# A decoder layer whose planner is given other costs, and whose gated stages get more groups of seven products

## The chip, the cores and the metric

The kernel runs on one core of a Trainium2 chip. The metric is device time in microseconds. Before the change it is 1747.77 us, the median of three runs (1747.45 to 1747.9). TensorE (PE in the profile) multiplies, VectorE (DVE) and ScalarE (ACT) prepare operands and finish results, SyncE (SP) issues the weight loads, GpSimd (POOL) issues the accumulating stores of the residual.

## The reference, cut to what matters

One layer on 256 tokens of width 2048, in float32: a gated feed-forward stage, a mixer of two kinds of attention, and a second gated stage. D_FF is 5632.

```
h = x + 0.5 * swiglu(rms_norm(x, g1), w_gate1, w_up1, w_down1)
u = rms_norm(h, g_mix);  proj = u @ w_in          # split into heads of two kinds
o = concat(rms_norm(o_fox), rms_norm(o_swa)) @ w_out;  h = h + o
y = h + 0.5 * swiglu(rms_norm(h, g2), w_gate2, w_up2, w_down2)
swiglu(x, g, u, d) = (silu(x @ g) * (x @ u)) @ d
```

## The kernel before, in words

**Products.** Every factor of a matrix product is split into a high and a low part, and a product is three matmuls of 128x512: high by high, low by high, high by low (`mm3`, L326 to L328). ScalarE makes the high part of a weight tile by a cast, VectorE the low part by subtracting the high one (L389).

**Units and groups.** `ffn()` is called once per gated stage. The 5632 columns are cut into 11 units of 512. A unit multiplies the normed input by the unit's gate and up weights in eight groups; a group is one pair of blocks of the input (pair 0 to 7) and one weight tile of 128x2048, 1 MB. After each unit but the first comes the previous unit's "down" block, four groups with the third weight matrix; the last two down blocks come together.

**Two kinds of group.** A plain group, D, is eight products: ScalarE casts the tile (L407), VectorE makes 2048 columns of low part (L389). A group of seven, S, computes the same 2x2 block product with seven products, in the manner of Strassen and Winograd. For it VectorE forms sums of weight blocks: an outer addition of 1024 columns (L437), two inner ones of 512 (L444, L445). ScalarE casts 1536 columns of the plain tile (L421) and twice 1024 of the sums (L423, L425). VectorE makes a low part of 1536 columns and one of 2048 (both L389). The first three products use the plain blocks, the other four the sums. The left side needs sums too, which `form_of` makes once per pair and stage, in the first unit in which that pair is in an S group: five steps on VectorE into `sqh` (L564 to L569), casts on ScalarE (L573, L574), then two low parts, `fu` and `u`. A unit with S groups ends with eight combination steps on VectorE (L626), then the gate (L641, L649) and the transposes and split of the result `hT` (L507, L389).

**Which unit has which kinds.** `UNITS` says it, one letter a group, the same for both stages: unit 0 is eight D, unit 1 "DDSSDSDD", unit 2 "DSSSSSDD", the other eight "SDSSSSSD". The S groups of a unit take the lowest pairs.

**What sets the order.** The code of a stage makes tasks, and `arrange` puts them in order, before anything is issued, by simulating the five engines with a cost for each task. `cast(n)` and `sub(n)` are the costs of a cast and an addition or subtraction of n columns, `LAG` the time from a task's end to its users' start; other costs are numbers in the code. A task is taken when its inputs are there and its buffers free, the earliest `due` first. Each engine then runs its list in the order found. The buffers of a stage are 3 raw tiles, 2 of sums, 5 of high and 5 of low parts.

**Vectors.** A tile `vec` of 128x226 with gains, biases and rotary factors is loaded at the start by ScalarE's queue (L256). Its first 64 columns are what the gated stages use, and the mixer uses the rest: the rotary tables (L938), the negated sinks `nsink` (L950), the forget bias and the gains of the other heads. SP loads the mixer's other constants, `mst`, at L881.

Of the kernel before, what the change touches and what calls it, by code (L numbers as in the profile page):

```python
# [9 lines left out]
F32 = mybir.dt.float32  # L10
# [7 lines left out]
P = 128  # L18
# [6 lines left out]
HD = 64  # L25
# [12 lines left out]
UNITS = ["D" * 8, "DDSSDSDD", "DSSSSSDD"] + ["SDSSSSSD"] * (NB - 3)  # L38
# [5 lines left out]
F2_ORDER += [(2, "whiy", F32R)] * (NHI - 2 - FREE2) + [(3, "wloy", F32R)] * (NLO - 2 - FREE2) + [(0, "rawy", F32)] * (NRAW - 3)  # L44

# [32 lines left out]
LAG = 0.06  # L78
# [3 lines left out]
def cast(n):  # L82
    return 0.2 + 0.00084 * n


def sub(n):
    return 0.16 + 0.00104 * n
# [9 lines left out]
def arrange(tasks, pools):  # L97
# [102 lines left out]
def hybrid_layer(ctx: ExitStack, tc: tile.TileContext, a: dict, out: bass.AP):  # L200
# [55 lines left out]
    nc.scalar.dma_start(vec, a["vec"])  # L256
# [101 lines left out]
    def ffn(pool, u, wgu, wd, slots, banks, rstd, held=None, first=None, lead=None, done=None, out=None):  # L358
# [58 lines left out]

        def seven(src):
# [49 lines left out]
        def group(kind, src, held, stat, need, form=None, pieces=1, last=False):  # L468

            new, w, free = seven(src) if kind == "S" else whole(src, pieces)  # L470
# [62 lines left out]
        def squares_of(ssq, c, need, due):  # L533

            ends = []
            for t in range(NT):
                q = task("act", 0.84, None, need[t], due, take={"sq": 1})
# [11 lines left out]
        count = [k.count("S") for k in UNITS]  # L549

        def form_of(p, need, due):

            tile_, over = fu[p], u(2 * p)[:, :, P:SEQ]
# [35 lines left out]
        def unit(b):  # L589

            kinds, ns = UNITS[b], count[b]
            pair = {"S": iter(range(ns)), "D": iter(range(ns, 8))}
            held, hs, sq3 = {}, [], []
            for n, kind in enumerate(kinds):
                p = next(pair[kind])
                if b == 0 and first is not None:
                    first[0](p, task, ready)
                if kind == "S" and p not in forms:
                    fresh[p] = len(main)
                    form_of(p, used[p] + [x for k in (2 * p, 2 * p + 1) for x in ready.get(k, ())], len(main) - 4)  # L600
# [18 lines left out]
            if ns:  # L619
# [4 lines left out]
                def step(o_, key, in1, op, need, due, free=True):  # L624
                    return task(
                        "dve", 0.69, lambda: tt(out=o_(), in0=bank_of(held[key]), in1=in1(), op=op), need + [held[key]["last"]], due,  # L626
# [12 lines left out]
            for t in range(NT):  # L639
                src = (lambda t=t: s_tile()[:, t, :]) if ns else (lambda t=t: bank_of(R(t, 0)))  # L640
                a = task("act", 0.73, lambda t=t, src=src: nc.scalar.activation(  # L641
# [7 lines left out]
                f = task("dve", 0.7, lambda t=t, src=src: stt(  # L649
# [9 lines left out]
            def finish(k, v, x):  # L659
# [6 lines left out]
                l = task("dve", 0.69, lambda: low(rows_tile()[:, :, 1, :], v(), rows_tile()[:, :, 0, :]), [c], due + 4)  # L666
# [12 lines left out]
        def down(blocks, final):  # L679
# [5 lines left out]
            for i, (cp, b, c) in enumerate(todo):  # L685
                final_of_cp = cp not in [x[0] for x in todo[i + 1 :]]
                if left[b] == 4:
# [3 lines left out]
                    "D", wd[cp][2 * b + c], held[cp], lambda k, t, b=b, c=c: halves(rows[b][:, 2 * c + k], t),  # L691
# [9 lines left out]
        def settle(cp, held, final, later):  # L701

            due, c0, ends = len(main), 2 * cp * 512, []
            for t in range(NT):
                if not final:
                    pair = []
                    for j in range(2):
                        def run(t=t, j=j, pair=pair, held=held):
# [3 lines left out]
                            "act", 0.63, run, [held[t, j]["last"]] + pair, due + t + 4 * j, take={"st": 1} if j == 0 else (),  # L712
# [101 lines left out]
    with tc.tile_pool(name="f1", bufs=1) as fp:  # L814
# [10 lines left out]
        def before(p, task, ready):  # L825
# [12 lines left out]
            for j in range(2):  # L838
                k = 2 * p + j
                gain = vec[:, V_G1 + k : V_G1 + k + 1]  # L840
                c = task("act", 0.46, lambda j=j, k=k, gain=gain: nc.scalar.mul(
                    u1(k)[:, 0, :], xs[i][:, p % 4, j], gain
                ), [ld], 8 * p - 4)
                l = task("dve", 0.48, lambda j=j, k=k, gain=gain: nc.vector.scalar_tensor_tensor(
# [33 lines left out]
    with tc.tile_pool(name="mix", bufs=1) as mp:  # L878
        ap_ = mp
        mst = mp.tile([P, C_END - C_ONE], F32, name="mst")  # L880
        nc.sync.dma_start(mst, a["cst"][:, C_ONE:])  # L881
        ones, tri = mst[:, :P], mst[:, C_TRI - C_ONE : C_TRI - C_ONE + P]
# [55 lines left out]
        def rope_tables(name, gcol):  # L938
            g = vec[:, gcol : gcol + HD]
# [10 lines left out]
        nc.vector.tensor_scalar_mul(nsink, vec[:, V_SINK : V_SINK + NH], -1.0)  # L950
# [93 lines left out]
        def fox_mm(hf, i):  # L1044
# [11 lines left out]
            out=z, in0=prs[:, :, 0:NH], in1=vec[:, V_BF : V_BF + NH].unsqueeze(1).broadcast_to([P, NT, NH]), op=ALU.add  # L1056
# [117 lines left out]
        def fox_rows(hf, i, pr, rf):  # L1174
# [3 lines left out]
            for t in range(NT):  # L1178
# [11 lines left out]
                for jj in range(2):  # L1190
                    bt = small_ps()
                    for j in range(4):
# [8 lines left out]
                        vec[0 : HD + 2, gcol : gcol + 1],  # L1201
# [85 lines left out]
    with tc.tile_pool(name="f2", bufs=1, reuse_waits=REUSE) as fp:  # L1287
        slots, fu = [[], [], [], []], []
        for i, nm, dt in F2_ORDER:
            if i == 4:  # L1290
                fu += [fp.tile([P, 3, 2, P], F32R, name="fu%d" % p) for p in range(max(k.count("S") for k in UNITS))]
# [90 lines left out]
```

## Time and profile before

| | us |
|---|---|
| median of three runs | 1747.77 |
| the profiled execution | 1747.29 |
| its span, first to last instruction | 1745.0 |
| TensorE busy | 1734.7 |
| VectorE busy | 1510.2 |
| ScalarE busy | 1058.4 |
| GpSimd busy | 73.8 |

The span is 2.29 us shorter than the execution's own time. Stage 1 runs from the start to about 700 us, the mixer to about 1055 us, stage 2 to the end. The granted TensorE clock is 1.000. A busy time is a sum of instruction durations with overlaps counted once; TensorE's matmuls overlap, so the distance from one start to the next is shorter than a duration. A row of a timeline gives the start from the span's beginning, the duration, the engine and line, output and inputs, and in brackets how long the engine had been idle and what ended that.

### The profile page before, as it was taken

The page shows a single profiled execution, that of the slowest core. Times are in us where ns is not written, and L with a number is a line of the kernel's source. Part 1 is how long each engine was busy: PE and PEld are TensorE (multiplying, and loading weights), DVE is VectorE, ACT ScalarE, POOL GpSimd, SP SyncE. Part 2 cuts the span into 40 slices and gives each one's busy share as a digit, 9 for nine tenths or more (in the row PEclk, how much of TensorE's full clock was granted, in tenths as well). Part 3 has the DMA queues.
Part 4 walks back from the last instruction along what each step waited for, and adds up shares of the span by engine and source line. Part 5 has one row for each costly group of instructions (what it writes and reads, how often), then busy time and mean ns, then how long its engine had stood idle before and what let it go on. Part 6 is the DMA issues. An engine that isn't in the chain of part 4 may idle for free.

```text
span 1745.0 us, 21056 instructions
## 1 busy us (share of the span) xinstructions
PE 1734.7 (99%) x8052; PEld 1444.1 (83%) x8052; DVE 1510.2 (87%) x1640; ACT 1058.4 (61%) x1217; POOL 73.8 (4%) x94
## 2 busy tenths in 40 slices
PE   9999999999999999999999999999999999999999
PEld 6888888888888888998788888888888888888887
DVE  7899999998999996668777769799999999999994
ACT  7566566666666654655766656556666566656661
POOL 0000000000000000000000000000000000000000
PEclk9999999999999999999999999999999999999999
DMA  9676677678678664564444456577678578667763
GB/s 345 221 234 237 215 247 246 212 241 250 229 220 266 227 237 154 166 210 153 139 146 138 135 191 241 201 209 241 217 227 259 220 233 265 215 226 246 256 214 121
DMA packets 73141, 377.49 MB, mean 216 GB/s; under 512 B 7760, under 2 KB 16464, under 8 KB 39504
## 3 DMA queue, kind: packets, MB, share of 16 engines
q1 hardware_dynamic: 62064, 337.09, 53.8%
q0 software_dynamic: 10688, 38.80, 11.5%
q8 instruction: 63, 1.03, 0.2%
q14 instruction: 38, 0.31, 0.1%
q10 hardware_dynamic: 288, 0.25, 0.0%
HBM read 336.27 MB, written 2.10 MB: 194 GB/s over the span
## 4 chain that ended last, share of the span: by engine, by line
PE 98%; DMA 1%; DVE 0%; ACT 0%; issue 0%; SPq 0%; DVEq 0%
PE acc L327 25%; PE acc L326 25%; PE acc L328 25%; PE sm L328 6%; PE sm L326 6%; PE sm L327 6%; PE acc L507 1%; PE sm L1025 1%; PE sc L1214 1%; DMA rawx<-in_wgu 1%; PE sm L1031 1%; PE sm L1193 0%; PE sm L507 0%; DMA raw<-in_wgu 0%; PE sc L1139 0%; PE sm L1032 0%
## 5 line engine op out<-in xcount | busy, mean ns | idle before, releaser
L326 PE MATMUL acc<-whi,u 128*128 128x512 f32 (+1 forms) x690 | 263.4, 383 | 0.9 <-DVE s L989 0.9
L327 PE MATMUL acc<-wlo,u 128*128 128x512 f32 (+1 forms) x690 | 263.4, 382 | 0.6 <-DVE wlo L389 0.5
L328 PE MATMUL acc<-whi,u 128*128 128x512 f32 (+1 forms) x690 | 262.0, 381 | 0.0
L243 DVE TENSOR_TENSOR wlo<-raw,whi 128x1024 fp32r<-128x1024 f32 (+1 forms) x112 | 128.9, 1154 | 75.1 <-ACT whi L242 74.5
L242 ACT CAST whi<-raw 128x1024 fp32r<-128x1024 f32 (+1 forms) x112 | 111.0, 991 | 96.8 <-PE acc L328 88.1
L389 DVE TENSOR_TENSOR wlo<-raw,whi 128x1536 fp32r<-128x1536 f32 (+3 forms) x73 | 142.1, 1949 | 8.8 <-ACT whi L407 8.7
L326 PEld LDWEIGHTS acc<-whi,u 128*128 128x128 f32 x690 | 129.4, 188 | 24.0 <-DVE s L989 1.3
L327 PEld LDWEIGHTS acc<-wlo,u 128*128 128x128 f32 x690 | 129.5, 188 | 23.4 <-DVE wlo L389 1.4
L328 PEld LDWEIGHTS acc<-whi,u 128*128 128x128 f32 x690 | 129.4, 188 | 22.1 <-issue 0.8
L710 ACT ACTIVATE st<-acc 128x512 f32<-128x512 f32 x109 | 65.5, 601 | 82.3 <-PE acc L328 81.2
L389 DVE TENSOR_TENSOR wloy<-raw,whiy 128x1536 fp32r<-128x1536 f32 (+1 forms) x55 | 110.2, 2004 | 5.5 <-ACT whiy L407 5.5
L718 POOL DMA_DIRECT2D h<-st x72 | 62.4, 867 | 1212.8 <-ACT st L710 1110.0
L389 DVE TENSOR_TENSOR wlox<-raw,whix 128x2048 fp32r<-128x2048 f32 (+1 forms) x52 | 109.5, 2111 | 1.0 <-ACT whix L407 1.0
L389 DVE TENSOR_TENSOR wlo<-sums,whi 128x2048 fp32r<-128x2048 f32 x45 | 102.9, 2286 | 8.3 <-ACT whi L425 8.3
L437 DVE TENSOR_TENSOR sums<-raw 128x1024 f32<-128x1024 f32 x76 | 92.6, 1219 | 14.9 <-DMA raw<-in_wgu 14.9
L407 ACT CAST whi<-raw 128x2048 fp32r<-128x2048 f32 (+2 forms) x43 | 75.3, 1752 | 36.1 <-DMA raw<-in_wd 15.7
L407 ACT CAST whix<-raw 128x2048 fp32r<-128x2048 f32 x35 | 66.9, 1911 | 39.4 <-DMA raw<-in_wd 11.8
L327 PE MATMUL acc<-wlox,u 128*128 128x512 f32 x223 | 86.9, 390 | 0.5 <-DVE wlox L389 0.5
L328 PE MATMUL acc<-whix,u 128*128 128x512 f32 x223 | 86.8, 389 | 0.0
L326 PE MATMUL acc<-whix,u 128*128 128x512 f32 x223 | 86.8, 389 | 0.0
L389 DVE TENSOR_TENSOR wloy<-sums,whiy 128x2048 fp32r<-128x2048 f32 x34 | 77.7, 2286 | 4.4 <-ACT whiy L425 4.4
L327 PE MATMUL acc<-wloy,u 128*128 128x512 f32 x209 | 81.4, 390 | 0.1
(340 smaller groups left out, 4526.5 us busy)
## 6 DMA issues: line engine op xcount, KB each, us to landing
raw<-in_wgu SPq DMA_DIRECT2D x109, 1024.0 KB, 5.1
raw<-in_wd SPq DMA_DIRECT2D x65, 1024.0 KB, 4.8
h<-st POOLq DMA_DIRECT2D x72, 512.0 KB, 6.0
rawy<-in_wgu SPq DMA_DIRECT2D x33, 1024.0 KB, 4.8
rawx<-in_wgu SPq DMA_DIRECT2D x32, 1024.0 KB, 5.8
raw<-in_wf SPq DMA_DIRECT2D x48, 512.0 KB, 3.8
raw<-in_wo SPq DMA_DIRECT2D x32, 512.0 KB, 3.4
raw<-in_ws SPq DMA_DIRECT2D x32, 388.0 KB, 3.5
```

The costliest lines, as they stand in the source:

```text
L242: nc.scalar.copy(hi, src)
L243: nc.vector.tensor_tensor(out=lo, in0=src, in1=hi.bitcast(F32), op=ALU.subtract)
L326: nc.tensor.matmul(o, lhsT=shi, rhs=mhi, start=start, stop=False)
L327: nc.tensor.matmul(o, lhsT=shi, rhs=mlo, start=False, stop=False)
L328: nc.tensor.matmul(o, lhsT=slo, rhs=mhi, start=False, stop=stop)
L389: tt(out=o_, in0=a, in1=f32(b), op=ALU.subtract)
L407: c.run = lambda raw=raw, hi=hi: nc.scalar.copy(hi(), raw())
L437: tt(out=sm()[:, :1024].rearrange("p (j n) -> p j n", j=2), in0=v[:, 0:3:2, :], in1=v[:, 3:4, :].broadcast_to([P, 2, 512]), op=ALU.add,)
L507: nc.tensor.transpose(bt[:, j * SEQ + t * P : j * SEQ + (t + 1) * P], src()[:, t, m], ident)
L710: nc.scalar.mul(st[:, j * 512 : j * 512 + 512], bank_of(held[t, j]), 0.5)
L718: nc.gpsimd.dma_start(h[:, t, c0 : c0 + 1024], st, accum_op=ALU.add)
L1025: nc.tensor.transpose(bt[:, j * P : (j + 1) * P], src[:, j, :], ident)
```

## The change

`UNITS` becomes one list per stage. In stage 1 unit 1 is "DDSSDSSD" and unit 2 "DSSSSSSD", one S more in each. In stage 2 unit 1 is "DSSDSSSD", two S more, and unit 2 "DSSSSSSD", one more. The planner's costs are lowered to the distance from start to start of the operations, `LAG` is raised, and tasks of POOL need no longer be taken in program order. `vec` is cut to 64 columns, and the other 162 are loaded at the mixer's start into a tile `own`, by SP right after `mst`. `DOWN`, `PAIRS` and the kind "L" are written so that nothing uses them otherwise than before. `PAD` moves addresses.

```diff
-UNITS = ["D" * 8, "DDSSDSDD", "DSSSSSDD"] + ["SDSSSSSD"] * (NB - 3)
+UNITS = [["D" * 8, x, "DSSSSSSD"] + ["SDSSSSSD"] * (NB - 3) for x in ("DDSSDSSD", "DSSDSSSD")]
+DOWN = "DDDD"
+PAIRS = [list(range(8)), list(range(8))]
...
-LAG = 0.06
+LAG = 0.13
 def cast(n):
-    return 0.2 + 0.00084 * n
+    return 0.04 + 0.00087 * n
 def sub(n):
-    return 0.16 + 0.00104 * n
+    return 0.07 + 0.00104 * n
...
-            some = left[:1] if e in ("sp", "pool") else [t for t in left if t.due <= pos + AHEAD]
+            some = left[:1] if e == "sp" else [t for t in left if t.due <= pos + AHEAD]
...
-    vec = keep.tile([P, V_END], F32, name="vec")
+    vec = keep.tile([P, V_BF], F32, name="vec")
-    hold.tile([P, 16], F32, name="pad")
+    hold.tile([P, PAD], F32, name="pad")
-    nc.scalar.dma_start(vec, a["vec"])
+    nc.scalar.dma_start(vec, a["vec"][:, :V_BF])
...
-                    c = task("act", 0.46, lambda j=j, dst=dst, gain=gain: nc.scalar.mul(dst[:, 0, :], v()[:, j], gain), [x], due)
-                    l = task("dve", 0.48, lambda j=j, dst=dst, gain=gain: stt(
+                    c = task("act", 0.37, lambda j=j, dst=dst, gain=gain: nc.scalar.mul(dst[:, 0, :], v()[:, j], gain), [x], due)
+                    l = task("dve", 0.39, lambda j=j, dst=dst, gain=gain: stt(
...
-                        "dve", 0.69, lambda: tt(out=o_(), in0=bank_of(held[key]), in1=in1(), op=op), need + [held[key]["last"]], due,
+                        "dve", 0.605, lambda: tt(out=o_(), in0=bank_of(held[key]), in1=in1(), op=op), need + [held[key]["last"]], due,
...
         nc.sync.dma_start(mst, a["cst"][:, C_ONE:])
+        own = mp.tile([P, V_END - V_BF], F32, name="own")
+        nc.sync.dma_start(own, a["vec"][:, V_BF:])
...
-        nc.vector.tensor_scalar_mul(nsink, vec[:, V_SINK : V_SINK + NH], -1.0)
+        nc.vector.tensor_scalar_mul(nsink, own[:, V_SINK - V_BF : V_SINK - V_BF + NH], -1.0)
```

On TensorE the list has 15 matmuls fewer. How VectorE's list moves at three places is shown by its rows: line, operation, output<-inputs, shape (the changed kernel's lines are 3 to 16 higher).

Stage 1, unit 1, from the first S group's outer addition on, before:

```order
L437 TENSOR_TENSOR sums<-raw 128x1024
L444 TENSOR_TENSOR sums<-sums,raw 128x512
L445 TENSOR_TENSOR sums<-sums,raw 128x512
L437 TENSOR_TENSOR sums<-rawx 128x1024
L389 TENSOR_TENSOR wlo<-raw,whi 128x1536
L389 TENSOR_TENSOR hT<-acc,hT 128x2x256 x2
L389 TENSOR_TENSOR wlo<-sums,whi 128x2048
L444 TENSOR_TENSOR sums<-sums,rawx 128x512
L445 TENSOR_TENSOR sums<-sums,rawx 128x512
L389 TENSOR_TENSOR wlox<-rawx,whix 128x1536
L437 TENSOR_TENSOR sums<-raw 128x1024
L389 TENSOR_TENSOR wlox<-sums,whix 128x2048
```

and of the change:

```order
L578 TENSOR_TENSOR sqh<-u 128x256 x2
L580 TENSOR_TENSOR sqh<-sqh 128x128
L581 TENSOR_TENSOR sqh<-sqh 128x128
L582 TENSOR_TENSOR sqh<-sqh 128x128
L583 TENSOR_TENSOR sqh<-sqh 128x128
L457 TENSOR_TENSOR sums<-sums,raw 128x512
L458 TENSOR_TENSOR sums<-sums,raw 128x512
L392 TENSOR_TENSOR hT<-sm,hT 128x2x256 x2
L392 TENSOR_TENSOR wlo<-raw,whi 128x1536
L392 TENSOR_TENSOR wlo<-sums,whi 128x2048
L450 TENSOR_TENSOR sums<-rawx 128x1024
L392 TENSOR_TENSOR fu<-sqh,fu 128x3x128
```

The five steps of pair 3's form now stand between the first group's outer and inner additions, and its low parts ahead of the second group's.

Stage 1, unit 2, the sixth and seventh groups, before:

```order
L437 TENSOR_TENSOR sums<-raw 128x1024
L389 TENSOR_TENSOR wlo<-sums,whi 128x2048
L444 TENSOR_TENSOR sums<-sums,raw 128x512
L445 TENSOR_TENSOR sums<-sums,raw 128x512
L389 TENSOR_TENSOR wlox<-raw,whix 128x1536
L389 TENSOR_TENSOR wlox<-sums,whix 128x2048
L389 TENSOR_TENSOR wlox<-rawx,whix 128x2048
```

and of the change:

```order
L450 TENSOR_TENSOR sums<-raw 128x1024
L392 TENSOR_TENSOR fu<-sqh,fu 128x3x128
L392 TENSOR_TENSOR u<-sqh,u 128x128
L457 TENSOR_TENSOR sums<-sums,raw 128x512
L458 TENSOR_TENSOR sums<-sums,raw 128x512
L450 TENSOR_TENSOR sums<-rawx 128x1024
L392 TENSOR_TENSOR wlox<-raw,whix 128x1536
L392 TENSOR_TENSOR wlox<-sums,whix 128x2048
L457 TENSOR_TENSOR sums<-sums,rawx 128x512
L458 TENSOR_TENSOR sums<-sums,rawx 128x512
L392 TENSOR_TENSOR wlo<-rawx,whi 128x1536
L392 TENSOR_TENSOR wlo<-sums,whi 128x2048
```

The plain low part of the seventh group (the last row before) has become an outer addition, two inner ones and two low parts, and the low parts of pair 5's form stand ahead of them.

The mixer's start, VectorE, of the change:

```order
L286 TENSOR_SCALAR rmy<-rmt 128x2
L966 TENSOR_SCALAR nsink<-own 128x16
L929 TENSOR_SCALAR cnt<-tmp 128x64
L291 TENSOR_TENSOR rmt<-rmy 128x2
L931 TENSOR_SCALAR part<-cnt 128x64
L246 TENSOR_TENSOR wlo<-raw,whi 128x2x388
```

The sinks are read from the new tile three rows ahead of a weight split; before, they stood eleven rows earlier, right behind the cast of the positions. SP's list there has one row more and is otherwise the same:

```order
L895 DMA mst<-in_cst 128x768
L897 DMA own<-in_vec 128x162
L240 DMA raw<-in_ws 128x2x388
```

The new load stands between the constants and the next weights.

More of the change, by code (lines that the diff above doesn't have):

```diff
@@ L44 @@
 F2_ORDER += [(2, "whiy", F32R)] * (NHI - 2 - FREE2) + [(3, "wloy", F32R)] * (NLO - 2 - FREE2) + [(0, "rawy", F32)] * (NRAW - 3)
+PAD = 184
 C_ID, C_INVF, C_ONE, C_TRI, C_MSK = 0, 128, 160, 288, 416
@@ L416, in whole, with added_low @@
             return new, [(by[i * 512 // n], lambda i=i: cols(i)) for i in range(4)], {3: [("hi", c0), ("lo", l0)]}
+        def added_low(src):
+            ld = task("sp", 2.9, lambda: nc.sync.dma_start(raw(), src), take={"raw": 1}, lag=2.3)
+            c = task("act", cast(2048), lambda: nc.scalar.copy(hi(), raw()), [ld], take={"hi": 1}, give=[("raw", ld)])
+            n = task("act", cast(2048), lambda: nc.scalar.mul(lo(), f32(hi()), -1.0), [c], take={"lo": 1})
+            a = task("pool", 0.9, lambda: nc.gpsimd.dma_start(lo(), src, accum_op=ALU.add), [n], lag=9)
+            raw, hi, lo = lambda: raws[ld.got["raw"][0]], lambda: his[c.got["hi"][0]], lambda: los[n.got["lo"][0]]
+            w = [([c, a], lambda i=i: (cols_of(hi())[i], cols_of(lo())[i])) for i in range(4)]
+            return [(ld, -45), (c, -20), (n, -20), (a, -20)], w, {3: [("hi", c), ("lo", n)]}
         def seven(src):
@@ L468, in group @@
         def group(kind, src, held, stat, need, form=None, pieces=1, last=False):
-            new, w, free = seven(src) if kind == "S" else whole(src, pieces)
+            new, w, free = seven(src) if kind == "S" else added_low(src) if kind == "L" else whole(src, pieces)
             n0 = len(main)
@@ L536, in squares_of @@
             for t in range(NT):
-                q = task("act", 0.84, None, need[t], due, take={"sq": 1})
+                q = task("act", 0.74, None, need[t], due, take={"sq": 1})
                 q.give.append(("sq", q))
@@ L548, in ffn @@
         forms = {}
-        count = [k.count("S") for k in UNITS]
+        units = UNITS[0 if first is not None else 1]
+        count, seven_of = [k.count("S") for k in units], PAIRS[0 if first is not None else 1]
         def form_of(p, need, due):
-            tile_, over = fu[p], u(2 * p)[:, :, P:SEQ]
+            tile_, over = fu[seven_of.index(p)], u(2 * p)[:, :, P:SEQ]
             def views(a):
@@ L589, in unit @@
         def unit(b):
-            kinds, ns = UNITS[b], count[b]
-            pair = {"S": iter(range(ns)), "D": iter(range(ns, 8))}
+            kinds, ns = units[b], count[b]
+            pair = {"S": iter(sorted(seven_of[:ns])), "D": iter(sorted(seven_of[ns:]))}
             held, hs, sq3 = {}, [], []
             for n, kind in enumerate(kinds):
-                p = next(pair[kind])
+                p = next(pair["D" if kind == "L" else kind])
                 if b == 0 and first is not None:
@@ L599, in unit @@
                     fresh[p] = len(main)
-                    form_of(p, used[p] + [x for k in (2 * p, 2 * p + 1) for x in ready.get(k, ())], len(main) - 4)
+                    form_of(p, used.get(p, []) + [x for k in (2 * p, 2 * p + 1) for x in ready.get(k, ())], len(main) - 4)
                 n0 = group(
@@ L640, in unit @@
                 src = (lambda t=t: s_tile()[:, t, :]) if ns else (lambda t=t: bank_of(R(t, 0)))
-                a = task("act", 0.73, lambda t=t, src=src: nc.scalar.activation(
+                a = task("act", 0.63, lambda t=t, src=src: nc.scalar.activation(
                     s_tile()[:, t, :], src(), AF.Silu, scale=rms[-1][:, t : t + 1]
@@ L648, in unit @@
                 src = up[t] if ns else (lambda t=t: bank_of(R(t, 1)))
-                f = task("dve", 0.7, lambda t=t, src=src: stt(
+                f = task("dve", 0.66, lambda t=t, src=src: stt(
                     out=s_tile()[:, t, :], in0=src(), scalar=rms[-1][:, t : t + 1], in1=s_tile()[:, t, :], op0=ALU.mult, op1=ALU.mult,
@@ L665, in finish @@
                 c = task("act", cast(512), lambda: nc.scalar.copy(rows_tile()[:, :, 0, :], v()), [x], due + 4)
-                l = task("dve", 0.69, lambda: low(rows_tile()[:, :, 1, :], v(), rows_tile()[:, :, 0, :]), [c], due + 4)
+                l = task("dve", 0.605, lambda: low(rows_tile()[:, :, 1, :], v(), rows_tile()[:, :, 0, :]), [c], due + 4)
                 row_ready[b, k // 2] = [c, l]
@@ L690, in down @@
                 group(
-                    "D", wd[cp][2 * b + c], held[cp], lambda k, t, b=b, c=c: halves(rows[b][:, 2 * c + k], t),
+                    "D" if final else DOWN[i], wd[cp][2 * b + c], held[cp], lambda k, t, b=b, c=c: halves(rows[b][:, 2 * c + k], t),
                     lambda k, b=b, c=c: row_ready[b, c], last=final_of_cp,
@@ L711, in settle @@
                         pair.append(task(
-                            "act", 0.63, run, [held[t, j]["last"]] + pair, due + t + 4 * j, take={"st": 1} if j == 0 else (),
+                            "act", 0.51, run, [held[t, j]["last"]] + pair, due + t + 4 * j, take={"st": 1} if j == 0 else (),
                             give=[("bank", held[t, j]["first"])],
@@ L840, in before @@
                 gain = vec[:, V_G1 + k : V_G1 + k + 1]
-                c = task("act", 0.46, lambda j=j, k=k, gain=gain: nc.scalar.mul(
+                c = task("act", 0.37, lambda j=j, k=k, gain=gain: nc.scalar.mul(
                     u1(k)[:, 0, :], xs[i][:, p % 4, j], gain
                 ), [ld], 8 * p - 4)
-                l = task("dve", 0.48, lambda j=j, k=k, gain=gain: nc.vector.scalar_tensor_tensor(
+                l = task("dve", 0.39, lambda j=j, k=k, gain=gain: nc.vector.scalar_tensor_tensor(
                     out=u1(k)[:, 1, :], in0=xs[i][:, p % 4, j], scalar=gain, in1=f32(u1(k)[:, 0, :]),
@@ L938, in rope_tables @@
         def rope_tables(name, gcol):
-            g = vec[:, gcol : gcol + HD]
+            g = own[:, gcol - V_BF : gcol - V_BF + HD]
             ga = g[:, 0:32].unsqueeze(1).broadcast_to([P, NT, 32])
@@ L1055, in hybrid_layer @@
         nc.vector.tensor_tensor(
-            out=z, in0=prs[:, :, 0:NH], in1=vec[:, V_BF : V_BF + NH].unsqueeze(1).broadcast_to([P, NT, NH]), op=ALU.add
+            out=z, in0=prs[:, :, 0:NH], in1=own[:, :NH].unsqueeze(1).broadcast_to([P, NT, NH]), op=ALU.add
         )
@@ L1200, in fox_rows @@
                         bt[0 : HD + 2, :].rearrange("p (j k) -> p j k", j=4),
-                        vec[0 : HD + 2, gcol : gcol + 1],
+                        own[0 : HD + 2, gcol - V_BF : gcol - V_BF + 1],
                     )
@@ L1290, in hybrid_layer @@
             if i == 4:
-                fu += [fp.tile([P, 3, 2, P], F32R, name="fu%d" % p) for p in range(max(k.count("S") for k in UNITS))]
+                fu += [fp.tile([P, 3, 2, P], F32R, name="fu%d" % p) for p in range(max(k.count("S") for k in UNITS[1]))]
             else:
```

## Prediction

> **What bounds the kernel now.** I read the page's busy shares and chain first, then TensorE's waits, then single rows of the two gated stages, because the change works there. Page, busy shares and chain of waits:
>
> ```profile
> span 1745.0 us, 21056 instructions
> PE 1734.7 (99%) x8052; PEld 1444.1 (83%) x8052; DVE 1510.2 (87%) x1640; ACT 1058.4 (61%) x1217; POOL 73.8 (4%) x94
> PE 98%; DMA 1%; DVE 0%; ACT 0%; issue 0%; SPq 0%; DVEq 0%
> ```
>
> TensorE is the path. Its waits over the whole execution (engine and line, what it waited for: us, times, longest):
>
> ```profile
> PE sm L823 <- ACT zero L820: 2.7, 1, 2.7
> PE sm L1193 <- ACT aug L1198: 1.0, 1, 1.0
> PE acc L326 <- DVE s L989: 0.9, 1, 0.9
> ...
> PE acc L327 <- DVE wlo L389: 0.5, 1, 0.5
> ```
>
> They lie at the start and in the mixer; the same view cut to 50 to 700 and to 1055 to 1740 us, which is nearly all of both gated stages, has no row at all. So there a product less is a gain of its whole length, as long as VectorE and ScalarE go on delivering split weights in time. That proviso is the whole question, since each new group of seven products gives them more to do.
>
> **What a product is worth.** TensorE's timeline in stage 1's unit 1, in unit 2, and in stage 2's unit 1 (start, duration, line, output<-inputs):
>
> ```profile
> 70.80 0.39 PE L326 MATMUL acc<-whix,u 128*128 128x512 f32 x1
> 71.03 0.39 PE L327 MATMUL acc<-wlox,u 128*128 128x512 f32 x1
> 71.48 0.39 PE L326 MATMUL acc<-whix,fu 128*128 128x512 f32 x1
> ...
> 146.72 0.39 PE L327 MATMUL sm<-wlox,u 128*128 128x512 f32 x1
> ...
> 1126.17 0.39 PE L327 MATMUL acc<-wloy,u 128*128 128x512 f32 x1
> ```
>
> From 70.80 to 71.48 the three matmuls of one product take 0.68 us (not 3 x 0.39: they overlap). Stage 1 gets one S group more in unit 1 and one in unit 2; stage 2 two in unit 1 and one in unit 2. That is five products fewer: 5 x 0.68 = **3.40 us less** on the path.
>
> **What an S group costs VectorE.** Its timeline: two S groups of stage 1, and a form of a pair in stage 2.
>
> ```profile
> 67.14 2.29 DVE L389 TENSOR_TENSOR wlox<-sums,whix 128x2048 fp32r<-128x2048 f32 x1 [0.82 <-ACT whix L425]
> 122.96 1.22 DVE L437 TENSOR_TENSOR sums<-raw 128x1024 f32<-128x1024 f32 x1
> 124.11 1.75 DVE L389 TENSOR_TENSOR wlox<-rawx,whix 128x1536 fp32r<-128x1536 f32 x1
> ...
> 134.31 0.69 DVE L444 TENSOR_TENSOR sums<-sums,raw 128x512 f32<-128x512 f32 x1
> 135.04 0.69 DVE L445 TENSOR_TENSOR sums<-sums,raw 128x512 f32<-128x512 f32 x1
> 135.65 1.75 DVE L389 TENSOR_TENSOR wlox<-raw,whix 128x1536 fp32r<-128x1536 f32 x1
> 137.31 2.28 DVE L389 TENSOR_TENSOR wlox<-sums,whix 128x2048 fp32r<-128x2048 f32 x1
> 139.52 2.29 DVE L389 TENSOR_TENSOR wlox<-rawx,whix 128x2048 fp32r<-128x2048 f32 x1
> ...
> 1078.62 0.55 DVE L389 TENSOR_TENSOR fu<-sqh,fu 128x384 fp32r<-128x384 f32 x1
> 1079.29 0.75 DVE L564 TENSOR_TENSOR sqh<-u 128x256 f32<-128x256 f32 x2
> ...
> 1081.02 2.29 DVE L389 TENSOR_TENSOR wlo<-rawy,whi 128x2048 fp32r<-128x2048 f32 x1
> ```
>
> I count from start to start, since that is what an operation keeps the next one from. The outer addition takes 124.11 - 122.96 = 1.15, the inner pair 135.65 - 134.31 = 1.34, the low part of 1536 columns 1.66, that of 2048 columns 139.52 - 137.31 = 2.21. An S group is 6.35 us of VectorE, a D group 2.2 (one low part), so each group changed adds about **4.15 us to VectorE** and takes 0.68 from TensorE. Once per pair comes the form of the left operand: 1081.02 - 1079.29 = 1.73 and 1079.29 - 1078.62 = 0.67, together 2.40 us. The change makes no more forms, it makes them a unit earlier: pair 3 in stage 1's unit 1 rather than unit 2, pair 5 in unit 2 rather than unit 3.
>
> The trace has 2.21 from start to start where the operation is shown for 2.28. The Trainium skill's "VectorE: DVE Perf Modes", section "The DRAIN you can't avoid", says that the next operation does not start until the pipe has emptied; read so, an S group costs 1.22 + 0.69 + 0.69 + 1.75 + 2.28 and a D group 2.28, and the late place below would come out about 0.6 us later and the time at 1745.4. The rows at 137.31 and 139.52, which depend on different weights, speak against it here.
>
> **Stage 1, unit 1.** The second S group's sums have their low part ready at 67.14 + 2.29 = 69.43, and TensorE takes it first at 71.03: 1.60 us in hand, the least of this stage's start. The form of pair 3 now stands ahead of it: + 2.40. The wait of 0.82 in that row is filled by it, as the form is VectorE work that does not need the cast waited for. 69.43 - 0.82 + 2.40 = 71.01 against 71.03. Just in time; I take 0 to 0.4 of waiting here.
>
> **Stage 1, unit 2.** The tightest place is its seventh group, D before and S now. Its low part ends at 139.52 + 2.29 = 141.81 and is first used at 146.72. Ahead of it VectorE gets unit 1's S group (4.15), pair 5's form (2.40) and this group's own (4.15): 152.5. TensorE needs it 0.68 earlier for the product gone in unit 1, and 2.04 later, since an S group's sums are used from its fourth product: 146.72 - 0.68 + 2.04 = 148.08. So VectorE is 4.4 us late unless it fills idle time. Idle it has: its waits from 53 to 142 us, and the load of both engines there (busy per window, then clock and DMA share).
>
> ```profile
> DVE wlox L389 <- ACT whix L425: 1.2, 2, 0.8
> DVE wlox L389 <- ACT whix L407: 1.0, 1, 1.0
> DVE fu L389 <- ACT fu L573: 0.7, 1, 0.7
> DVE s L626 <- PE acc L328: 0.5, 1, 0.5
> ...
> 62.30:94.70 32.40, 32.40 (x145) 26.84 (x144) 29.87 (x23) 19.39 (x14) 0.00 (x0) 1.00 0.68 249
> 94.70:141.70 47.00, 47.00 (x213) 39.03 (x212) 45.58 (x49) 30.30 (x33) 3.61 (x4) 1.00 0.70 214
> ```
>
> 3.4 us of waits, nearly all for ScalarE's casts, and ScalarE is busy 19.39 of 32.40 and 30.30 of 47.00. All filled: 4.4 - 3.4 = 1.0 late, and less by what unit 1 itself held TensorE up. None filled: 4.4. A pure sum of the new order's pitches, with no wait and no gap, ends at about 148.2, 0.1 late. I take **0.45 us** for both places, nearer the low bound: the waits are for casts of an engine with a third of its time free, and the changed order sets other VectorE work (the form, the next outer addition) in front of them. The bounds are 0 and 4.4. From unit 3 on VectorE has pair 5's form (2.40) less to make, and no unit is changed there.
>
> **Stage 2.** Rows of its unit 1, VectorE:
>
> ```profile
> 1094.72 0.75 DVE L649 SCALAR_TENSOR_TENSOR s<-sm,rmy,s 128x512 f32<-128x512 f32 x1 [1.28 <-PE sm L328]
> 1102.07 2.29 DVE L389 TENSOR_TENSOR wlo<-sums,whi 128x2048 fp32r<-128x2048 f32 x1 [1.27 <-ACT whi L425]
> 1108.42 2.29 DVE L389 TENSOR_TENSOR wlo<-rawy,whi 128x2048 fp32r<-128x2048 f32 x1 [4.05 <-ACT whi L407]
> 1115.22 2.29 DVE L389 TENSOR_TENSOR wloy<-raw,whiy 128x2048 fp32r<-128x2048 f32 x1 [0.61 <-ACT whiy L407]
> ```
>
> The last is the seventh group, which becomes S: ready at 1117.51, used from 1126.17, 8.66 us in hand. Added before it: two S groups (8.3) and the forms of pairs 3 and 4 (4.8), 13.1 us; the need moves by - 0.68 + 2.04 = + 1.36. In hand are 8.66 + 1.36 + the four waits 7.21 = 17.2. That covers it with 4 us left; with no wait filled 3.1 us would be missing. I take **0**: the 4.05 is VectorE far ahead of its buffers, not a cast that lags.
>
> **Start.** The table of vectors is cut from 226 to 64 columns. ScalarE's first scaling waits for it, and the DMA engines are the bound of the first 20 us:
>
> ```profile
> 3.89 0.91 ACT L841 ACTIVATE u<-xs,vec 128x256 fp32r<-128x256 f32 x2 [1.21 <-DMA vec<-in_vec]
> ...
> 0.00:20.00 20.00, 16.16 (x61) 10.65 (x62) 10.65 (x16) 12.94 (x18) 0.20 (x4) 1.00 0.89 327
> ```
>
> 226 columns of 4 bytes in 128 rows are 116 KB, at 327 GB/s 0.35 us, of which 162/226, 0.25 us, is no longer moved ahead of the weights. From 0 to 0.25, I take **0.1**: the rows moved are as many, only shorter. On this the Trainium skill ("DMA: Bandwidth & Descriptors", section "Specifications") asks at least 512 B per transfer for line rate. Rows of 904 B become rows of 256 B; by it the saving would be nil and the time 1744.9. No row here has this load at both sizes.
>
> **Mixer.** The cut columns are loaded by a new SP transfer right behind the mixer's constants, and one small VectorE operation that reads them (L950, negated sinks) comes early:
>
> ```profile
> 700.53 0.35 SPq L881 DMA_DIRECT2D mst<-in_cst  x1
> 704.53 0.54 SPq L237 DMA_DIRECT2D raw<-in_ws  x1
> ...
> 701.22 0.17 DVE L950 TENSOR_SCALAR nsink<-vec 128x16 f32<-128x16 f32 x1
> ...
> 703.53 0.97 DVE L243 TENSOR_TENSOR wlo<-raw,whi 128x776 fp32r<-128x776 f32 x1
> ...
> mst<-in_cst SPq DMA_DIRECT2D x1, 384.0 KB, 3.1
> ```
>
> Issued at about 700.9 and landing like the constants 3.1 us later, the columns are there at 704.0; the operation now stands three places ahead of the weight split at 703.53, at about 703.0. VectorE works its list in order, so that split, the row-norm steps behind it and then TensorE's next weights are held up to 1.0 us. SP issues its next weight load only at 704.53, so the queue is not delayed. Weight splits are ahead of use here by more than that as far as I can follow them, some of the scaled operands by less. From 0 to 1.0, I take **0.1**.
>
> **Sum.** - 3.40 + 0.45 + 0 - 0.1 + 0.1 = - 2.95 us. The profiled execution took 1747.29 (span 1745.0 and 2.29 outside), 0.48 under the median; it would go to 1744.3 (span about 1742.0), and the median of 1747.77 to **1744.8**.
>
> **Rivals.** *VectorE late (the other side).* In unit 2 of stage 1 the waits for ScalarE are not filled, because ScalarE casts in the same order and its own work grows too: the whole 4.4 comes, and - 3.40 + 4.4 + 0 = + 1.0, **1748.8**, slower than before. It decides from the point where less than 1.0 of the 3.4 us of waits is filled. If stage 2 went the same way, 3.1 more: 1751.9. For it: VectorE is busy 45.58 of 47.00. Against it: its waits are short and spread, and ScalarE has slack.
> *Sinks wait in the mixer.* The whole 1.0 us reaches TensorE: **1745.7**. For it: the landing time; against it: one operation, once.
> *Full gain.* No new wait, the whole 0.25 at the start: - 3.65, **1744.1**. For it: the pure pitch sum is only 0.1 late.
> *The change doesn't do what it says*: other costs in the planner reorder steady units so that VectorE, busy 87% of the span, is late in many of them; a lateness of 0.45, as taken above for one place, in each of the 16 later units would be 7.2 us, **1752**. For it: in those units some 25 of each 60 VectorE operations change places. Against it: they do so with near neighbours, and no wait of TensorE stands there to start from.
>
> **How the numbers follow.** A measurement here can tell 0.2%, 3.5 us, from no change, so faster means up to 1744.27. Forecast (1744.3 to 1745.6) 0.52; full gain, about 1744.1, 0.26; sinks 0.05; VectorE late within 1747 to 1750 0.10; the planner's reordering or both stages late, over 1751, 0.07. Faster then is the full gain and the forecast's lower edge, 0.32; slower 0.07; the same the rest, 0.61. The range, 1743.8 to 1747.4, leaves out about one in seven above, where VectorE is late in full, and little below. The likeliest case's own is 1744.0 to 1745.6.
>
> **What would show it.** Fifteen matmuls fewer at an unchanged 0.68 per product; TensorE's waits between 60 and 75 and around 146 to 150 us: none or under 1 us for a low part (L389's successor) says the fill holds, over 3 says the first rival. In stage 2 no wait at all. The first product still at about 6.4 us. In the mixer, a wait of the negated sinks for their own load of about 1 us, and none of TensorE's just behind it. A span under 1741.3 or over 1744.6 would make the forecast wrong, and a TensorE wait in the steady units would make the reasoning wrong whatever the time.

## The result

The changed kernel takes **1770.32 us** (median; 1766.47 to 1773.06), the kernel before 1747.61 in the same runs: a ratio of 1.0129, 95% interval 1.0109 to 1.0148. It is slower by some 22.7 us, where 2.95 us less were forecast; it lies far over the top of the range.

The page of the changed kernel, busy shares and chain, and TensorE's waits over the whole execution (who waited for whom: us in total, times, longest):

```profile
span 1767.3 us, 21061 instructions
PE 1737.3 (98%) x8037; PEld 1439.9 (81%) x8037; DVE 1530.6 (87%) x1660; ACT 1055.9 (60%) x1227; POOL 73.9 (4%) x94
issue 49%; PE 31%; DVE 10%; DMA 5%; POOL 2%; ACT 2%; SPq 0%; POOLq 0%; ACTq 0%; DVEq 0%
```

```profile
PE acc L520 <- DVE s L663: 13.3, 11, 1.7
PE sm L520 <- DVE s L663: 5.8, 4, 1.6
PE sm L837 <- ACT zero L834: 2.7, 1, 2.7
PE sm L1209 <- ACT aug L1214: 1.0, 1, 1.0
```

Fifteen matmuls are gone as planned. The first two rows are new: the transposes at a unit's end (L520, L507 before) wait for the second gate product (`s`, L663), 19.1 us in 15 times. Before, no transpose waited for it, and from 50 us to 1740 us TensorE had no wait at all in either gated stage. The share of busy time hides the loss: 99% became 98%.

**One unit's end.** ScalarE, VectorE and TensorE of the changed kernel around 230 to 290 us, and TensorE again one unit later. The number in brackets is the idle time before the row and what ended it.

```profile
230.45 0.60 ACT L724 ACTIVATE st<-acc 128x512 f32<-128x512 f32 x1
230.94 1.06 ACT L438 CAST whi<-sums 128x1024 fp32r<-128x1024 f32 x1
231.88 0.61 ACT L724 ACTIVATE st<-sm 128x512 f32<-128x512 f32 x1
232.37 0.61 ACT L724 ACTIVATE st<-acc 128x512 f32<-128x512 f32 x1
232.84 0.62 ACT L724 ACTIVATE st<-sm 128x512 f32<-128x512 f32 x1
...
242.45 1.09 ACT L724 ACTIVATE st<-acc 128x512 f32<-128x512 f32 x2 [4.70 <-DMA h<-st]
245.89 1.09 ACT L724 ACTIVATE st<-acc 128x512 f32<-128x512 f32 x2 [2.35 <-DMA h<-st]
246.86 1.05 ACT L436 CAST whix<-sums 128x1024 fp32r<-128x1024 f32 x1
247.80 1.06 ACT L438 CAST whix<-sums 128x1024 fp32r<-128x1024 f32 x1
```

```profile
248.89 2.29 DVE L392 TENSOR_TENSOR wlox<-sums,whix 128x2048 fp32r<-128x2048 f32 x1 [4.04 <-ACT whix L438]
...
286.54 2.28 DVE L392 TENSOR_TENSOR wlo<-raw,whi 128x2048 fp32r<-128x2048 f32 x1
288.74 0.74 DVE L663 SCALAR_TENSOR_TENSOR s<-sqh,rmy,s 128x512 f32<-128x512 f32 x1
```

```profile
287.70 0.28 PE L520 MATMUL sm<-cst,s 128*128 128x128 f32 x1
289.53 0.55 PE L520 MATMUL sm<-cst,s 128*128 128x128 f32 x3 [1.55 <-DVE s L663]
...
351.60 0.27 PE L520 MATMUL sm<-cst,s 128*128 128x128 f32 x1
353.27 0.55 PE L520 MATMUL sm<-cst,s 128*128 128x128 f32 x3 [1.39 <-DVE s L663]
```

Read it from the top. A down block's results are scaled by ScalarE into one of two buffers `st` (L724) and added to the residual by a store of GpSimd. The second half's copies, at 242.45 and 245.89, find both buffers still being stored and wait 4.70 and 2.35 us. Behind them in ScalarE's list are the casts at 246.86 and 247.80, and VectorE waits 4.04 us for these. VectorE does not make that up: the second gate product begins at 288.74, and TensorE, which came to its transposes at 287.70, stands 1.55 us. From one unit's transposes to the next it is 351.60 - 287.70 = 63.9 us.

The same places before (ScalarE, VectorE, TensorE):

```profile
238.29 0.60 ACT L710 ACTIVATE st<-acc 128x512 f32<-128x512 f32 x1 [1.24 <-PE acc L328]
239.66 0.60 ACT L710 ACTIVATE st<-sm 128x512 f32<-128x512 f32 x1 [0.77 <-PE sm L328]
...
286.33 0.75 DVE L649 SCALAR_TENSOR_TENSOR s<-sqh,rmy,s 128x512 f32<-128x512 f32 x1
...
289.73 1.03 PE L507 MATMUL acc<-cst,s 128*128 128x128 f32 x8
...
351.82 0.60 PE L507 MATMUL acc<-cst,s 128*128 128x128 f32 x4
```

There the copies wait for TensorE, the buffers being free (over the whole execution ScalarE waited 2.3 us for stores); the gate product ends at 287.08, 2.65 us ahead of the transposes, and a unit takes 62.09 us. Over the whole execution ScalarE's waits for stores, and the stores from issue to landing (page, DMA issues: x count, KB each, us), the changed kernel first, the kernel before last:

```profile
ACT st L724 <- DMA h<-st: 100.7, 30, 5.2
...
h<-st POOLq DMA_DIRECT2D x72, 512.0 KB, 9.4
```

```profile
h<-st POOLq DMA_DIRECT2D x72, 512.0 KB, 6.0
```

The planner reckons 0.9 us for the issue and 7 us until a store's buffer is free, 7.9 together. Before, the median of 6.0 us fitted in that. Now it is 9.4, and the plan, which knows nothing of it, sets the next copies too early in ScalarE's list.

### The profile page after: what moved, and what is told of

It reads as the page before. It is cut to its first block, busy times and chain, and to the rows that moved or that the text cites. A ratio compares the mean times of both kernels' runs of the same rounds, so it can differ in the third digit from the quotient of the medians.

```text
span 1767.3 us, 21061 instructions
## 1 busy us (share of the span) xinstructions
PE 1737.3 (98%) x8037; PEld 1439.9 (81%) x8037; DVE 1530.6 (87%) x1660; ACT 1055.9 (60%) x1227; POOL 73.9 (4%) x94
## 3 DMA queue, kind: packets, MB, share of 16 engines
q0 software_dynamic: 10688, 38.80, 11.1%
## 4 chain that ended last, share of the span: by engine, by line
issue 49%; PE 31%; DVE 10%; DMA 5%; POOL 2%; ACT 2%; SPq 0%; POOLq 0%; ACTq 0%; DVEq 0%
PE acc L329 8%; PE acc L330 8%; PE acc L331 8%; DVE wlox L392 3%; DVE wlo L392 2%; POOL h L732 2%; DMA h<-st 2%; DMA rawx<-in_wd 1%; DVE sums L450 1%; DVE wloy L392 1%; PE sm L330 1%; PE sm L329 1%; PE sm L331 1%; DMA raw<-in_wd 1%; PE sm L1041 1%
## 5 line engine op out<-in xcount | busy, mean ns | idle before, releaser
L392 DVE TENSOR_TENSOR wlo<-raw,whi 128x1536 fp32r<-128x1536 f32 (+3 forms) x76 | 146.8, 1934 | 6.9 <-ACT whi L410 6.8
L724 ACT ACTIVATE st<-acc 128x512 f32<-128x512 f32 x109 | 61.7, 601 | 94.4 <-DMA h<-st 78.6
L392 DVE TENSOR_TENSOR wloy<-raw,whiy 128x1536 fp32r<-128x1536 f32 (+1 forms) x52 | 104.3, 2008 | 3.5 <-ACT whiy L410 3.5
L392 DVE TENSOR_TENSOR wloy<-sums,whiy 128x2048 fp32r<-128x2048 f32 x37 | 84.5, 2285 | 21.1 <-ACT whiy L438 21.1
L392 DVE TENSOR_TENSOR wlox<-sums,whix 128x2048 fp32r<-128x2048 f32 x34 | 77.7, 2285 | 19.9 <-ACT whix L438 19.9
```

What stands on the lines that cost most here:

```text
L392: tt(out=o_, in0=a, in1=f32(b), op=ALU.subtract)
L724: nc.scalar.mul(st[:, j * 512 : j * 512 + 512], bank_of(held[t, j]), 0.5)
```

## The experiments

There are two questions. Is it the new costs or the added groups of seven? "New costs" stands here for all that changed in the planner, `LAG` and POOL's free order included; no run separates these. And by what way do they cost: does the plan put the transposes too early whatever the stores do (theory 1), do the stores block ScalarE and everything follows (theory 2), or have the added groups used up VectorE's lead (theory 3)?

**Old costs, new units.** `LAG`, `cast`, `sub`, every other cost and POOL's program order as before; two of the lines:

```diff
-LAG = 0.13
+LAG = 0.06
...
-    return 0.07 + 0.00104 * n
+    return 0.16 + 0.00104 * n
```

> The changed kernel with all the planner's numbers as before (costs, LAG, POOL in program order); the new lists of units and the split vector tile stay. Theory 1 (the lower costs make the plan think the gate product ready earlier than it is, so the transposes stand too early in TensorE's list and wait there in each unit): no wait of the transposes, and the five products saved are the gain, about 1744.5 us. Theory 2 (in the new order ScalarE is blocked by the residual stores, whose buffers come free later than the plan has them, which starves VectorE): about 1744.5 too, since the old order has no such block. Theory 3 (the added groups of seven use up VectorE's lead, and the planner's numbers do little): still 1766 to 1772.

Measured: 1755.0 us (1752.93 to 1756.82), ratio 1.0042 (1.003 to 1.0055). No wait of the transposes for the gate, so the new costs are what brings that one. But the expected gain did not come either: no theory had this. TensorE's waits from 130 to 160 us, stage 1's unit 2:

```profile
PE acc L330 <- DVE wlo L392: 1.9, 1, 1.9
PE acc L330 <- DVE wlox L392: 1.4, 1, 1.4
```

This is the prediction's first rival, in the old order: with the old costs the added groups make VectorE late in unit 2 (3.3 us of waits; the rival had 4.4). The stores were late here too: they land in 9.8 us (median), and ScalarE waits 54.0 us for them. So the added groups alone, without the new costs, already lengthen the stores, in units whose own groups did not change.

**New costs, old units.**

```diff
-UNITS = [["D" * 8, x, "DSSSSSSD"] + ["SDSSSSSD"] * (NB - 3) for x in ("DDSSDSSD", "DSSDSSSD")]
+UNITS = [["D" * 8, "DDSSDSDD", "DSSSSSDD"] + ["SDSSSSSD"] * (NB - 3)] * 2
```

> The changed kernel with the lists of units as before in both stages; the new costs stay. Theories 1 and 2: the waits of the transposes for the gate product stay at 1 to 2 us in most of the later units, 15 to 19 us in all, and the time is 1765 to 1775. Theory 3: without the added groups the lead is back, and the time is 1746 to 1750.

Measured: 1763.48 us, ratio 1.0089 (1.0076 to 1.0103), a little under the range of theories 1 and 2. The transposes wait 12.8 us, ScalarE 87.2 us for stores, which land in 9.3 us. Theory 3 falls as the main cause: without the added groups most of the loss is there.

**Transposes later in the plan.**

```diff
-                ), [a, v[t] if ns else R(t, 1)["last"]], due + 9 if ns else due + 2 * t, lag=1.5)
+                ), [a, v[t] if ns else R(t, 1)["last"]], due + 9 if ns else due + 2 * t, lag=6.0)
```

> The changed kernel, where the plan alone reckons with 6.0 us instead of 1.5 from the end of the gate product to its use by the transposes. Theory 1: the transposes move some 4 us later in TensorE's list, the waits of 19 us go, and nothing else is late: 1744 to 1748. Theory 2: the transposes' waits go, but ScalarE is still blocked for about 100 us by the stores, VectorE is still late, and TensorE waits for low parts instead: 1755 to 1768.

Measured: 1759.2 us, ratio 1.0074 (1.0059 to 1.009), which is in theory 2's range, though not in the way it said: ScalarE's waits for stores fell to 54.4 us, where it had expected about 100 still. TensorE's waits:

```profile
PE sm L329 <- DVE hT L392: 4.3, 1, 4.3
PE acc L330 <- DVE wlo L392: 2.8, 3, 1.3
...
PE acc L329 <- DVE hT L392: 2.4, 1, 2.4
PE acc L330 <- DVE wlox L392: 1.1, 2, 0.6
```

The transposes' waits for the gate are gone, and the later units run at 62.09 us again. What is lost now is elsewhere: low parts in the first units, and `hT`, which comes too late where the next down block follows at once, 4.3 us at the very end. So a wrong place of the transposes is one link of the loss; this run does not say what makes it wrong.

**Stores longer in the plan.** One number, the time for which the plan keeps a store's buffer busy (the line is cut at its start).

```diff
- ... due + 8, give=[("st", pair[0])], lag=7)
+ ... due + 8, give=[("st", pair[0])], lag=11)
```

> The changed kernel, where the plan alone reckons with 11 us instead of 7 for a residual store to land. Theory 2: ScalarE's waits for the stores (100.7 us in the changed kernel) fall below 20 us, VectorE is in time, and the time is 1744 to 1750. Theory 1: the stores' waits may fall, but the gate product is still planned too early, and 10 us or more of the transposes' waits stay: 1758 to 1770.

Measured: 1746.39 us (1745.24 to 1748.06), ratio 0.9994 (0.9985 to 1.0003): 24 us less than the changed kernel from one number. The transposes' waits are gone. Theory 2 holds, and theory 1 as an independent cause falls, since the low costs are all still there. One part of what it expected missed: ScalarE's waits for the stores stayed at 47.5 us, not under 20, and the stores still land in 9.4 us. ScalarE and VectorE at the same place show how that can be:

```profile
239.42 1.09 ACT L724 ACTIVATE st<-acc 128x512 f32<-128x512 f32 x2 [3.07 <-DMA h<-st]
240.39 1.05 ACT L436 CAST whix<-sums 128x1024 fp32r<-128x1024 f32 x1
241.62 1.05 ACT L438 CAST whix<-sums 128x1024 fp32r<-128x1024 f32 x1 [0.18 <-PE acc L331]
242.82 1.09 ACT L724 ACTIVATE st<-acc 128x512 f32<-128x512 f32 x2
```

```profile
242.71 2.29 DVE L392 TENSOR_TENSOR wlox<-sums,whix 128x2048 fp32r<-128x2048 f32 x1 [0.89 <-ACT whix L438]
```

The two casts that VectorE needs now stand between the pairs of copies, not behind both. ScalarE still waits, but VectorE only 0.89 us instead of 4.04. What counted was not ScalarE's wait but what stood behind it.

**Shorter stores, nothing else moved.** The runs above change lists. This one leaves every engine's list as it is in the changed kernel and makes only the stores smaller; three quarters of the residual's sums are left out, so its output is not the layer's.

```diff
-  nc.gpsimd.dma_start(h[:, t, c0 : c0 + 1024], st, accum_op=ALU.add)
+  nc.gpsimd.dma_start(h[:, t, c0 : c0 + 256], st[:, :256], accum_op=ALU.add)
```

> The changed kernel with every engine's list as it is; only each residual store adds 256 of its 1024 columns, so that it lands sooner (three quarters of both stages' residual are left out). Theory 2 (the stores' late landing blocks ScalarE, and all else follows): ScalarE's waits for stores fall from 100.7 us to under 20, the transposes' waits of 19.1 us go to under 3, and the time is 1743 to 1748. Theory 1 (the lower costs place the transposes too early whatever the stores do): 12 us or more of the transposes' waits stay, 1760 or more.

Measured: 1745.4 us (1744.67 to 1745.95), ratio 0.9986 (0.9977 to 0.9995). The stores land in 5.0 us, ScalarE has no row of waits for them left, and the transposes none for the gate. ScalarE's rows:

```profile
237.72 0.60 ACT L724 ACTIVATE st<-acc 128x512 f32<-128x512 f32 x1 [1.24 <-PE acc L331]
239.09 0.60 ACT L724 ACTIVATE st<-acc 128x512 f32<-128x512 f32 x1 [0.77 <-PE acc L331]
...
```

The copies wait for TensorE again, as before the change. The same lists in which the transposes lost 19.1 us lose nothing when the stores land in time. That settles theory 2 against theory 1.

**Old units, longer stores.** The two edits shown above for the units and for the store.

> The new costs with the lists of units as before, and the plan's 11 us for a residual store. If the new costs hurt only by setting ScalarE's copies for the stores too early, the 12.8 us of the transposes' waits go and the time falls from 1763.5 to 1747.5 to 1749.5 (the time before, plus 0.95 for the slow output products). If the lower costs as such place the transposes too early, it stays above 1755.

Measured: 1748.09 us, ratio 1.0002 (0.9993 to 1.0011). The new costs hurt by the stores alone; without that they change nothing that can be measured.

**Old costs, longer stores.** The old costs as in the first experiment, and 11 us for a store.

> The new lists of units with all the planner's old costs, but 11 us for a residual store. In the kernel with the old costs (1755.0) stage 1's unit 2 waited 4.1 us for low parts, and later units some 0.5 to 1.2 us each, 4 us together. If the stores cause only the later waits, 1750 to 1752 is left; if they cause both, 1745 to 1747; if neither, 1755.

Measured: 1749.98 us, ratio 1.0013 (1.0004 to 1.0022). Five less than with 7 us, and unit 2's late low part still there (1.9 us of TensorE's wait, of 3.3): the stores cause the later waits, the old order most of the one in unit 2. So the new costs were of use there: with them unit 2 is in time, below.

**The vector tile alone.** Old costs, old units; every list is that of before but for the new load and the moved sinks.

> The planner's numbers and the lists of units as before: the split of the vector tile is all that is left of the change. All engines' lists are those of before but for the added load and the moved sinks. By the address theory 1748.6 us (0.95 more, all of it in the output products from about 1000 to 1060 us), and residual stores land in 6 us as before. If the split also disturbs the stores, their landing is 9 us and the time above 1750.

Measured: 1748.27 us, ratio 1.0003 (0.9994 to 1.0012), stores 6.2 us. In time it can't be told from before, but its trace shows a loss that every kernel with the split has, told in the next two.

**A wider tile for the cut columns.** The changed kernel with 11 us for a store, and this:

```diff
-        own = mp.tile([P, V_END - V_BF], F32, name="own")
+        own = mp.tile([P, 176], F32, name="own")[:, : V_END - V_BF]
```

> The kernel with the plan's 11 us for a residual store, and the tile of the mixer's cut columns widened from 162 to 176 columns (648 to 704 bytes a row, nothing read from the added ones), so that the mixer's later tiles begin at a multiple of 64 bytes again. In every run so far the 192 output products whose stationary operand comes from the tile oTf went at 233 ns from start to start instead of 227, which cost 0.95 us. Theory A (that tile's address, 32 bytes off a multiple of 64, slows the matmuls): back to 227 ns, 0.95 us less than the kernel with 11 us alone, about 1745.4 us. Theory B (something else, traffic or heat, slows them): still 233 ns and 1746.4 us.

Measured: 1745.2 us (1744.56 to 1749.95), ratio 0.9989 (0.998 to 0.9998). Output products by groups of the whole execution (count, busy us, mean ns): before the change, then 648 bytes a row with 11 us for a store, then 704:

```profile
L326 PE MATMUL acc<-whi,oTf 128*128 128x512 f32 x64 | 25.2, 393 | 0.0
L327 PE MATMUL acc<-wlo,oTf 128*128 128x512 f32 x64 | 25.0, 391 | 0.0
L328 PE MATMUL acc<-whi,oTf 128*128 128x512 f32 x64 | 24.9, 389 | 0.0
```

```profile
L330 PE MATMUL acc<-wlo,oTf 128*128 128x512 f32 x64 | 25.5, 398 | 0.0
L329 PE MATMUL acc<-whi,oTf 128*128 128x512 f32 x64 | 25.4, 397 | 0.0
L331 PE MATMUL acc<-whi,oTf 128*128 128x512 f32 x64 | 25.3, 396 | 0.0
```

```profile
L329 PE MATMUL acc<-whi,oTf 128*128 128x512 f32 x64 | 25.4, 397 | 0.0
L330 PE MATMUL acc<-wlo,oTf 128*128 128x512 f32 x64 | 25.1, 392 | 0.0
L331 PE MATMUL acc<-whi,oTf 128*128 128x512 f32 x64 | 25.0, 391 | 0.0
```

The products do follow the tile's size, and so, most likely, the address of the tiles behind it. 704 bytes, where the expectation had all three groups back, give back most of two.

**A tile of 1024 bytes a row.** The same edit with 256 columns.

> 11 us for a store in the plan, and the mixer's new tile 1024 bytes a row, so that the later tiles stand where they stood before, moved by 1024 bytes. The kernel with 704 bytes went from 0.95 to about 0.3 us too slow over the output products. Address theory: the output products as before (L329's group back from 397 to 393 ns), 0.3 us less, 1744.9. Otherwise 1745.2 as with 704.

Measured: 1746.34 us (1743.95 to 1749.8), ratio 0.9989 (0.998 to 0.9998). In the trace as expected: the groups of the output products are at 393, 391 and 389 ns, to the ns those of before, and from the first of these products to the last it takes 46.93 us as before. In time nothing is shown (1744.9 was expected): this kernel's runs spread over 6 us, and the profiled one had a wait of 1.2 us for a copy that was itself behind a store.

**14 us for a store.** As the last, with `lag=14`.

> As the kernel with the 1024-byte tile, but 14 us for a store in the plan. The waits of ScalarE for stores that are left at 11 us (47 to 51 us) cost TensorE nothing there, so no gain is expected: 1744.4 to 1746. If they still cost something, the time falls below 1744.4; if a plan with too long a store holds buffers back, over 1747.

Measured: 1752.71 us, ratio 1.0027 (1.0017 to 1.0038), and steady, 1752.28 to 1753.04. ScalarE has no wait for a store at all here, the stores land in 6.3 us, and it is 6 us slower than with 11. TensorE waits for the copies instead (2.8 us in two waits), and nearly every later unit takes 62.43 us instead of 62.09, which over 14 units is some 5 of the 6 us. That the plan holds the copies back, and with them the product buffers, is the likely reason; no run shows it. It is the third of the expectations: too long a store in the plan costs as well.

**Stage 2's units alone.** As the kernel with 1024 bytes and 11 us, stage 1's units as before.

> As the kernel with the 1024-byte tile and 11 us, but stage 1's units as before, so three products saved instead of five. By the products alone 1.36 us more than that kernel, 1746.3; if stage 1's late low parts and start eat its gain, as its trace has it (0.6 of 1.36 us seen), about 0.6 more, 1745.5.

Measured: 1745.87 us (1744.7 to 1749.21), ratio 0.9991 (0.9982 to 1.0). Not told apart from five products saved; the spread is as large as what was looked for.

The fastest version that computes the whole layer is, by its median, the changed kernel with 11 us for a store and the tile of 704 bytes: 1745.2 us, 2.5 us (0.14%) under the kernel before, and 25 under the changed one. The versions with 11 us and 1024 bytes lie within its spread.

## Why the prediction was wrong

**The products: right.** 15 matmuls fewer, 0.68 us each product. The four runs in which the stores no longer block and all five products are saved (the quarter stores, and 11 us with three sizes of the tile) come out 1.3 to 2.5 us under before. 3.4 less what each loses in the output products (1.2 to nothing, see the end) would be 2.2 to 3.4, so up to 1.8 us is not seen in one of them and is not assigned.

**Low parts in stage 1: right.** The two tight places of the prediction, VectorE and TensorE of the changed kernel:

```profile
68.45 2.29 DVE L392 TENSOR_TENSOR wlox<-sums,whix 128x2048 fp32r<-128x2048 f32 x1
...
145.48 2.28 DVE L392 TENSOR_TENSOR wlo<-sums,whi 128x2048 fp32r<-128x2048 f32 x1
```

```profile
71.10 0.39 PE L330 MATMUL acc<-wlox,u 128*128 128x512 f32 x1
...
148.15 0.39 PE L330 MATMUL acc<-wlo,u 128*128 128x512 f32 x1
```

Unit 1's sums were ready at 70.74 (predicted 71.01) and unit 2's at 147.76 (pitch sum 148.2), each 0.4 us ahead of use. The 0.45 us taken there was not lost. The first rival, VectorE late in unit 2, was real in the order of the old costs alone.

**The step that failed: "From unit 3 on VectorE has pair 5's form (2.40) less to make, and no unit is changed there."** The lists of these units did change, by the planner's costs, and by the added groups too (with the old costs their stores landed in 9.8 us). One of these units took 63.9 us instead of 62.09. I had seen that some 25 of each 60 VectorE operations change places and put it aside as "near neighbours", in a rival with a chance of 0.07 together with another. That rival named the right victim, VectorE late in the steady units, but not the cause, and its time, 1752, was too low: it took 0.45 us a unit, and TensorE's waits measured 1.3 us on average in 15 units. What I did not follow was ScalarE's list, and in it an operation whose wait is set by neither VectorE nor TensorE but by a transfer: the copy into `st`. The plan's 7.9 us for a store was in the code, the 6.0 us in the page: a reserve of 1.9 us. No term of the sum had the stores; they were put at nothing without a reason, and they landed in 9.4.

**The account.** The span grew by 22.3 us, with 3.4 saved: 25.7 lost. The transposes' waits are 19.1. From start to start the 15 pauses sum to 23.1 us where 15 unbroken steps take about 0.1 each, so some 21.6 with what restarting costs. The output products are 1.2. The other 3 us are not assigned row by row.

**Start.** 0.1 less was taken. The vectors came 0.1 us sooner (ScalarE's first scaling at 3.79 instead of 3.89), but the first product began later, 6.62 instead of 6.47: TensorE's opening row of ten matmuls on zeros lasts until then. The products behind it came 0.18 us sooner, until one that waits for a low part, at 13.46 instead of 13.37; from there on unit 0 runs 0.07 us late. No gain. In the traces of other runs with the same cut the same place lies between 0.3 sooner and 0.8 later, so a term of 0.1 could not be read from one trace.

**Mixer, sinks.** VectorE did wait, less than the 1.0 us bounded:

```profile
714.28 0.17 DVE L966 TENSOR_SCALAR nsink<-own 128x16 f32<-128x16 f32 x1 [0.69 <-DMA own<-in_vec]
```

TensorE's 388-column products behind it take 69.42 us from first to last start in both kernels (700.34 to 769.76 before, 710.79 to 780.21 after): the wait was covered, and the 0.1 was nothing.

**Stage 2.** No wait for a low part, as predicted; its loss is the same block by stores as in stage 1.

## What to carry to other kernels

Where a planner fixes the order, its costs are also margins. Making them exact for the engines leaves the transfers' costs as the only guesses, and here these lengthened from 6.0 to 9.4 us when the order changed; compare each planned transfer with its measured landing before trusting a new plan, and look at what stands behind the waiting instruction, not at how long it waits. When every list shifts a little, follow every engine for one steady unit, the copying engine too: a group with no wait before can become the bound.

## What the runs showed that was not expected

A 512-KB accumulating store issued by GpSimd lands in 6.0 us (median) in one order and 9.4 us in another, with the same sizes and counts. By issue and landing of each transfer, in stage 1's later units: before, the stores took 4.6 to 6.7 us, one of them 8.8, mostly with 0.4 to 1.2 weight loads in flight on average; in the changed kernel 8.7 to 12.0 with 1.0 to 1.4. There the first two stores of a unit also follow each other in 1.0 us, where before they were 3.6 apart, so the second store is a rival. With 14 us in the plan two stores 2.3 us apart took 6.2 to 7.3 with 0.5 to 0.7 loads beside them. With the old costs and the new units the first two are 3.6 us apart as before and took 8.9 to 11.1; the fourth store of a unit, with another store in flight for a tenth of its time and 1.6 to 1.9 loads, took 9.6 to 10.8. So it is the weight loads beside a store, more than the second store, that go with its length; no run moves the loads alone. The count of loads is not all of it: the third store of those same units landed in 4.8 to 5.4 us with 1.1 to 1.5 loads.

The packets of the DMA queues show where the time goes at one place. In the changed kernel the stores issued at 232.85 and 233.82 move nothing until 237.0; all packets from 232.9 to 237.0 are of the loads' queue, where a load issued at 233.18, behind the first store, is on its way. Before, the store issued at 228.79 begins to move its bytes at about 231.2.

The output products, matmuls whose stationary operand is the tile `oTf`, took 397, 398 and 396 ns on average (by group) where the new tile ahead of it has 648 bytes a row, 397, 392 and 391 with 704, and 393, 391 and 389 with 1024, as before the change, with no wait shown. From the first to the last start that is 48.10 us with 648 bytes and 46.93 before: 1.17 us over 192 products, not the 0.95 of the expectations. These kernels differ in where the tiles behind the new one begin, `oTf` among them, but the traces show no addresses: that its place against some boundary is the cause is likely, and which boundary stays open.
